# Second attention: one rounding and one subtraction for both heads, the halves moved by transfers

## The chip, the cores and the metric

The kernel runs on one core of a Trainium2 chip. The metric is the device time of one execution in microseconds; lower is better.

## What is computed

One inference step of a one-layer decoder: a prompt of 1024 rows and 8 sample rows with a paged cache of 8192 positions each. What matters here is the causal attention of the prompt with a forget gate, 8 heads of width 64:

```python
def fox_attend(q, k, v, cq, ck, qpos, kpos):
    s = jnp.einsum('bqhd,bkhd->bhqk', q, k).astype(jnp.float32) * (ATT_HEAD_DIM ** -0.5)
    s = s + (cq.astype(jnp.float32).transpose(0, 2, 1)[:, :, :, None]
             - ck.astype(jnp.float32).transpose(0, 2, 1)[:, :, None, :])
    s = jnp.where(kpos[None, :] <= qpos[:, None], s, -jnp.inf)
    p = jax.nn.softmax(s, axis=-1).astype(v.dtype)
    return jnp.einsum('bhqk,bkhd->bqhd', p, v)
```

Around it stand an input projection, a gating branch, an output projection, cross-attention into 256 memory tokens and a gated MLP with a convolution, for the prompt and for the samples.

## The kernel before

The prompt is worked in two halves of 512 rows. After the input projections (`p1`) comes the first attention (`attention(0)`: rows 0 to 511), then the second (`attention(1)`: rows 512 to 1023 against all 1024 keys), then for each half the merge, the output projection, cross-attention and the MLP. The samples' work, above all the reading of 128 pages of keys and 128 of values (L1420 and L1482, issued on POOL), is strewn into the prompt's by a pacing loop; DVE multiplies and reduces the key pages (in the attentions in quarters, L1427 and L1428), PE multiplies the value pages (L1488).

Matrices in float32 are split for PE into a rounded part h (type fp32r) and a rest l = x - h. For the scores, queries and keys of a head are laid out so that two matmuls do three products: `qq[:, 0, :]` holds the rounded queries in partitions 0 to 63 and their rests in 64 to 127, and `ka` holds the rounded keys twice, in both halves of the partitions (L807). `qq[:, 1, :]` holds the rounded queries again in 0 to 63, `kb` the keys' rests there, and partitions 64 to 67 of both carry the forget sums, loaded from `cq_d` and `ck_d` (L809).

An attention goes over four pairs of heads. `load` fetches a pair's queries (`qn`, one buffer), keys (`kn`) and values (`vn`) on SP's queue; in the second attention `kn` is a tile of the pool `t2` (7 buffers, shared with the outputs, some of the turned probabilities, and others). `setup` is a generator with one stop: the first step transposes the queries of both heads at once into one PSUM bank (L750) and rounds (ACT, L757), copies (POOL, L758) and subtracts (DVE, L774) head by head; the second does the same for keys (L779, L784, L785, L788). In the PSUM bank head 0 lies in partitions 0 to 63 and head 1 in 64 to 127. The first attention stores the split keys in `ks_d` in memory (L791, L792), and the second loads them from there for its first 512 keys (L769, L770, on SP), so that its setup only splits the 512 new ones. The operands `qq`, `ka` and `kb` are tiles of the pool `u` (18 buffers).

For a pair, `scores` is called eight times (two blocks of query rows, two heads, two row tiles); each call makes the scores on PE in column chunks, the row maximum on DVE (L813, L816), and the exponential on ACT (L814, L817; in the second attention into a `wr` tile, the buffers that also take weights). `turn` transposes the probabilities (PE L836, ACT L843 or DVE L841), `values` multiplies them with the values (L852), `back` transposes the result (L872, L874). The next pair's `load` is called after the first call of `scores`, its `setup` begins after the fourth, and its second step follows one call later.

Each engine takes its instructions in order. The order is made when the program is built, by a scheduler that uses an estimate of each instruction's time; `tc.issue_after` and `behind` add edges to it (`calm()` puts the rounding after the latest exponential). Transfers on SP's queue take turns on eight completion semaphores, and a transfer is issued only when the one eight before it, on the same semaphore, has landed.

Of the kernel before, what the change touches and what calls it, by code (L numbers as in the profile page):

```python
# [7 lines left out]
F32 = mybir.dt.float32  # L8
F32R = mybir.dt.float32r
BF16 = mybir.dt.bfloat16  # L10
I32 = mybir.dt.int32
AF = mybir.ActivationFunctionType
ALU = mybir.AluOpType
# [65 lines left out]
def build(nc, tc, ctx, a, phases=None):  # L79
# [27 lines left out]
    def nm(s):  # L107
        cnt[0] += 1
        return f"{s}_{cnt[0]}"

    def U(shape, dt=F32):
        n = 1
        for s in shape[1:]:
            n *= s
        t = upool.tile([P, UW], dt, tag="u", bufs=NU, name=nm("u"))[:, :n]
        if len(shape) == 3:
            t = t.rearrange("p (a b) -> p a b", b=shape[2])
        return t

    def T2(n=512, dt=F32):  # L120
        return tpool.tile([P, 512], dt, tag="t2", bufs=NT, name=nm("t2"))[:, :n]
# [604 lines left out]
    def attention(hf, late=None, at=3):  # L726
# [3 lines left out]
        def load(hp):  # L730
# [9 lines left out]
            nc.sync.dma_start(vn, v_d[: nk * P, cs].rearrange("(i p) c -> p i c", p=P))  # L740
            return qn, kn, vn

        def setup(hp, qn, kn, vn):


            calm = lambda: tc.issue_after(lastexp[0]) if lastexp else nullcontext()
            with behind(ENG.PE):
                tr = (MS, BB, BA)[SB]()
                for i in range(4):
                    nc.tensor.transpose(tr[:, i * P : (i + 1) * P], qn[:, i, :], ident)  # L750
            qab, ka, kb = [], [], []
            for j in range(2):
                h = hp * 2 + j
                rows = slice(64 * j, 64 * j + 64)
                qq = U([P, 2, 512], F32R)
                with calm():
                    nc.scalar.activation(qq[0:64, 0, :], tr[rows, :], AF.Copy)  # L757
                nc.gpsimd.tensor_copy(qq[0:64, 1, :], qq[0:64, 0, :].bitcast(F32))  # L758
                nc.gpsimd.dma_start(qq[64:68, 1, :], cq_d[h, :, hf * 512 : (hf + 1) * 512])
                qab.append(qq)  # L760
                if hf == 0:
                    kab = U([P, 2, 512], F32R)
                    ka.append(kab[:, 0, :])
                    kb.append(kab[:, 1, :])
                else:
                    ka.append(U([P, nk * P], F32R))
                    kb.append(U([P, nk * P], F32R))
                    for r in range(2):
                        nc.sync.dma_start(ka[j][64 * r : 64 * r + 64, 0:512].bitcast(F32), ks_d[h, :, 0, :])  # L769
                    nc.sync.dma_start(kb[j][0:64, 0:512].bitcast(F32), ks_d[h, :, 1, :])  # L770
                nc.gpsimd.dma_start(kb[j][64:68, :], ck_d[h, :, : nk * P])
            for j, qq in enumerate(qab):
                rows = slice(64 * j, 64 * j + 64)
                nc.vector.tensor_tensor(qq[64:128, 0, :], tr[rows, :], qq[0:64, 0, :].bitcast(F32), op=ALU.subtract)  # L774
            yield
            with behind(ENG.PE):
                tr = (MS, BB, BA)[SB]()
                for i in range(4):
                    nc.tensor.transpose(tr[:, i * P : (i + 1) * P], kn[:, i, :], ident)  # L779
            s = slice(hf * 512, hf * 512 + 512)  # L780
            for j in range(2):
                rows = slice(64 * j, 64 * j + 64)
                with calm():
                    nc.scalar.activation(ka[j][0:64, s], tr[rows, :], AF.Copy)  # L784
                nc.gpsimd.tensor_copy(ka[j][64:128, s], ka[j][0:64, s].bitcast(F32))  # L785
            for j in range(2):
                rows = slice(64 * j, 64 * j + 64)
                nc.vector.tensor_tensor(kb[j][0:64, s], tr[rows, :], ka[j][0:64, s].bitcast(F32), op=ALU.subtract)  # L788
            if hf == 0:
                for j in range(2):  # L790
                    nc.gpsimd.dma_start(ks_d[hp * 2 + j, :, 0, :], ka[j][0:64, :].bitcast(F32))  # L791
                    nc.gpsimd.dma_start(ks_d[hp * 2 + j, :, 1, :], kb[j][0:64, :].bitcast(F32))  # L792
            got.append((qab, ka, kb, vn))
# [92 lines left out]

        got = []
        first = setup(0, *load(0))
        if hf:
            next(first)  # L890
# [5 lines left out]
        for hp in range(4):  # L896
# [5 lines left out]
            for blk in range(2):  # L902
# [6 lines left out]
                for j in range(2):  # L909
                    for ii in range(2):  # L910
                        p_ = scores(qkv, ls, blk, j, ii)
                        if ii == 0:
                            pt.append(
                                [
                                    (U([P, 4, 256]) if nkt - g > 2 else T2(512).rearrange("p (a b) -> p a b", b=256))
                                    for g in range(0, nkt, 4)
                                ]
                            )
                        queue.append(partial(turn, p_, pt[j], nkt - 1 + ii, ii))
                        if j == 1 and ii == 1:  # L920

                            def fin(*args):
                                r = values(*args)
                                queue.insert(min(BKQ, len(queue)), partial(back, *r))

                            queue.append(partial(fin, qkv, ls, pt, hp, blk))
                        drain(LA[hf])
                        yield 1.8
                        if hp < 3 and (blk, j, ii) == LD[hf]:
                            raw = load(hp + 1)  # L930
                        if hp < 3 and (blk, j, ii) == ST[hf]:
                            nxt = setup(hp + 1, *raw)
                        if nxt:
                            next(nxt, None)
                            yield 1
# [425 lines left out]
    def behind(e):  # L1361

        return tc.issue_after(last[e]) if e in last else nullcontext()
# [480 lines left out]
    def prompt():  # L1844
# [4 lines left out]

        got, ahead = [], []  # L1850
        att1 = attention(1, lambda: got.append(merge_in(0)))
        att0, fill0 = attention(0, (lambda: next(att1)) if LT < 4 else None, LT), fill()

        def early():
# [170 lines left out]
```

## Time and profile before

| | us |
|---|---|
| median of 3 runs | 1805.22 |
| lowest and highest | 1799.28, 1807.2 |
| profiled execution, device time | 1804.14 |
| its span, first to last instruction | 1802.1 |
| PE busy in the span | 1737.0 |
| DVE busy | 1398.2 |
| ACT busy | 736.4 |
| POOL busy | 506.6 |

The mean granted TensorE clock is 0.991 of full speed. The page has the busy share of each engine, the span in 40 slices, the DMA queues, the chain of work that ended last and the costliest groups. Finer views answer for a stretch, a line or a tile. In them a group's row gives the line, engine, operation, output and inputs, the count, and the duration of one in ns; a wait's row gives who waited for whom, the total in us, the count and the longest; a timeline row gives the start, the length, the instruction and, in brackets, the idle time before it with what ended it. A row of a timeline with x2 stands for two instructions one after the other.

### The profile page before, as it was taken

The page shows a single profiled execution, that of the slowest core. Times are in us where ns is not written, and L with a number is a line of the kernel's source. Part 1 is how long each engine was busy: PE and PEld are TensorE (multiplying, and loading weights), DVE is VectorE, ACT ScalarE, POOL GpSimd, SP SyncE. Part 2 cuts the span into 40 slices and gives each one's busy share as a digit, 9 for nine tenths or more (in the row PEclk, how much of TensorE's full clock was granted, in tenths as well). Part 3 has the DMA queues.
Part 4 walks back from the last instruction along what each step waited for, and adds up shares of the span by engine and source line. Part 5 has one row for each costly group of instructions (what it writes and reads, how often), then busy time and mean ns, then how long its engine had stood idle before and what let it go on. Part 6 is the DMA issues. An engine that isn't in the chain of part 4 may idle for free.

```text
span 1802.1 us, 25097 instructions
## 1 busy us (share of the span) xinstructions
PE 1737.0 (96%) x9637; PEld 1287.2 (71%) x9637; DVE 1398.2 (78%) x1729; ACT 736.4 (41%) x1378; POOL 506.6 (28%) x461
## 2 busy tenths in 40 slices
PE   8999999878999999999999999999989999999997
PEld 5887777555677667777777777776666778767875
DVE  4689658988788986999999999887875549855344
ACT  6332265465643635333333244336353323332332
POOL 1252333433123332332322223343422112002110
PEclk9999999999999999999999999999999999999999
DMA  8886888786697985778788778988879687568982
GB/s 296 301 298 226 300 317 329 265 273 212 223 407 277 355 331 217 290 291 341 296 305 309 290 302 321 377 304 325 308 276 338 224 297 249 185 260 299 357 312 82
DMA packets 157074, 521.06 MB, mean 289 GB/s; under 512 B 20874, under 2 KB 40842, under 8 KB 124186
## 3 DMA queue, kind: packets, MB, share of 16 engines
q0 software_dynamic: 57168, 341.14, 49.8%
q1 hardware_dynamic: 92874, 165.73, 26.7%
q10 hardware_dynamic: 6912, 12.59, 1.9%
q8 instruction: 76, 1.25, 0.3%
q14 instruction: 44, 0.36, 0.1%
HBM read 495.47 MB, written 23.93 MB: 288 GB/s over the span
## 4 chain that ended last, share of the span: by engine, by line
PE 47%; DMA 11%; issue 8%; DVE 6%; POOL 2%; ACT 1%; POOLq 0%; DVEq 0%
DMA kv<-cache_v,io 7%; PE ba L272 6%; PE ba L274 6%; PE ba L273 6%; PE dv L1488 3%; PE bb L272 3%; PE bb L274 3%; PE bb L273 3%; DMA kv<-cache_k,io 2%; DVE s L1440 2%; DVE kv L1436 1%; PE dv L331 1%; PE dv L1764 1%; POOL kv L1482 1%; POOL kv L1420 1%
## 5 line engine op out<-in xcount | busy, mean ns | idle before, releaser
L235 ACT ACTIVATE wh<-wr 128x1024 fp32r<-128x1024 f32 (+2 forms) x220 | 228.9, 1044 | 421.5 <-PE ba L273 138.8
L236 DVE TENSOR_TENSOR wl<-wr,wh 128x1024 fp32r<-128x1024 f32 (+2 forms) x220 | 262.9, 1199 | 172.6 <-PE ba L274 57.7
L1420 POOL DMA_INDIRECT kv<-cache_k,io x128 | 199.2, 1556 | 570.9 <-DVE s L1440 325.3
L1436 DVE TENSOR_TENSOR kv<-kv,d 128x1024 f32<-128x1024 f32 (+1 forms) x156 | 258.1, 1681 | 24.7 <-DMA kv<-cache_k,io 24.7
L1440 DVE TENSOR_REDUCE s<-kv 128x16 f32<-128x1024 f32 (+1 forms) x156 | 258.1, 1672 | 0.0
L1482 POOL DMA_INDIRECT kv<-cache_v,io x128 | 168.5, 1317 | 254.9 <-PE dv L1488 177.5
L272 PE MATMUL ba<-u,wh 128*128 128x512 f32 x528 | 209.3, 397 | 0.0
L273 PE MATMUL ba<-u,wh 128*128 128x512 f32 x528 | 208.8, 396 | 0.5 <-DVE u L239 0.5
L274 PE MATMUL ba<-u,wl 128*128 128x512 f32 x528 | 208.8, 396 | 0.0
L272 PE MATMUL ba<-wh,u 128*128 128x512 f32 (+1 forms) x495 | 186.4, 379 | 2.6 <-ACT u L235 2.6
L273 PE MATMUL ba<-wl,u 128*128 128x512 f32 (+1 forms) x495 | 185.1, 375 | 1.2 <-DVE wl L236 1.2
L274 PE MATMUL ba<-wh,u 128*128 128x512 f32 (+1 forms) x495 | 183.2, 375 | 0.0
L1488 PE MATMUL dv<-kv,s 128*32 128x512 f32 x1024 | 127.7, 606 | 3.6 <-DMA kv<-cache_v,io 3.5
L272 PEld LDWEIGHTS ba<-u,wh 128*128 128x128 f32 x528 | 99.5, 188 | 27.2 <-issue 5.6
L274 PEld LDWEIGHTS ba<-u,wl 128*128 128x128 f32 x528 | 99.3, 188 | 26.5 <-issue 4.0
L273 PEld LDWEIGHTS ba<-u,wh 128*128 128x128 f32 x528 | 99.3, 188 | 25.8 <-issue 3.1
L272 PEld LDWEIGHTS ba<-wh,u 128*128 128x128 f32 x495 | 93.0, 188 | 27.0 <-issue 6.5
L272 PE MATMUL bb<-u,wh 128*128 128x512 f32 x272 | 108.7, 400 | 0.0
L274 PE MATMUL bb<-u,wl 128*128 128x512 f32 x272 | 107.8, 397 | 0.0
L273 PE MATMUL bb<-u,wh 128*128 128x512 f32 x272 | 107.6, 396 | 0.0
L273 PEld LDWEIGHTS ba<-wl,u 128*128 128x128 f32 x495 | 93.0, 188 | 20.0 <-DVE wl L236 1.9
L274 PEld LDWEIGHTS ba<-wh,u 128*128 128x128 f32 x495 | 92.9, 188 | 19.5 <-issue 1.6
(445 smaller groups left out, 3313.8 us busy)
## 6 DMA issues: line engine op xcount, KB each, us to landing
wr<-w_up SPq DMA_DIRECT2D x88, 512.0 KB
kv<-w_up POOLq DMA_DIRECT2D x22, 1024.0 KB, 7.6
wr<-w_down SPq DMA_DIRECT2D x40, 512.0 KB
kv<-w_down POOLq DMA_DIRECT2D x11, 1024.0 KB, 8.3
wr<-w_in SPq DMA_DIRECT2D x16, 512.0 KB
wr<-w_o SPq DMA_DIRECT2D x16, 512.0 KB
wr<-w_cq SPq DMA_DIRECT2D x16, 512.0 KB
wr<-w_co SPq DMA_DIRECT2D x16, 512.0 KB
```

The source lines that it names most:

```text
L235: nc.scalar.activation(h, src, AF.Copy)
L236: nc.vector.tensor_tensor(l, src, h.bitcast(F32), op=ALU.subtract)
L272: mmul(out, sh, mh, start=(i == 0), stop=False)
L273: mmul(out, sh, ml, start=False, stop=False)
L274: mmul(out, sl, mh, start=False, stop=(i == n - 1))
L331: mmul(ps[32 * j : 32 * j + 32, :w], xT[:, k, :] if nk == 8 else xT[:, k * 8 : k * 8 + 32], raw[:, q, j * w : (j + 1) * w], start=(k == 0) ...
L1420: nc.gpsimd.indirect_dma_start(kv, None, a["cache_k"], off(kidx[:, b, ch : ch + 1]))
L1436: nc.vector.tensor_tensor(kvv[:, i : i + m, :], kvv[:, i : i + m, :], qb.unsqueeze(1).broadcast_to((P, m, 512)), op=ALU.mult)
L1440: nc.vector.tensor_reduce(s[:, ch * 4 + i : ch * 4 + i + m, :].rearrange("p k h -> p (k h)"), kvv[:, i : i + m, :].rearrange("p k (h d) -> ...
L1482: nc.gpsimd.indirect_dma_start(kv, None, a["cache_v"], off(kidx[:, b, ch : ch + 1]))
L1488: mmul(dv[32 * j : 32 * j + 32, :], s[:, ch * 4 : ch * 4 + 4, :].rearrange("p k h -> p (k h)"), kvv[:, j, :], start=(ch == 1), stop=(ch == ...
L1764: mmul(ps[32 * j : 32 * j + 32, :P], xsT[:, k, :], rvs[j // 2][:, k, j % 2, :], start=(k == 0), stop=(k == 7), tile_position=(0, 32 * j),)
```

## The change

In the second attention only (`hf` is 1), `setup` no longer works head by head. A new helper `halves` rounds the whole PSUM bank, both heads, in one ACT instruction over 128 partitions, back into the tile that held the rows before the transpose (`qn` or `kn`), and subtracts in one DVE instruction into a new tile of the pool `t2`. Twelve transfers a pair on SP's queue, six for queries and six for keys, each of 64 partitions of 512 elements, bring the parts to their places in `qq`, `ka` and `kb`. The copies on POOL are gone there. The first attention is as it was.

```diff
+        def halves(tr, rows_, calm):
+
+            h = rows_.rearrange("p i c -> p (i c)")
+            with calm():
+                nc.scalar.activation(h.bitcast(F32R), tr, AF.Copy)
+            l = T2(512, F32R)
+            nc.vector.tensor_tensor(l, tr, h, op=ALU.subtract)
+            return h, l.bitcast(F32)
+
         def setup(hp, qn, kn, vn):
...
             qab, ka, kb = [], [], []
+            if hf:
+                qh, ql = halves(tr, qn, calm)
             for j in range(2):
                 h = hp * 2 + j
                 rows = slice(64 * j, 64 * j + 64)
                 qq = U([P, 2, 512], F32R)
-                with calm():
-                    nc.scalar.activation(qq[0:64, 0, :], tr[rows, :], AF.Copy)
-                nc.gpsimd.tensor_copy(qq[0:64, 1, :], qq[0:64, 0, :].bitcast(F32))
+                if hf:
+                    for dst, part in ((qq[0:64, 0, :], qh), (qq[0:64, 1, :], qh), (qq[64:128, 0, :], ql)):
+                        nc.sync.dma_start(dst.bitcast(F32), part[rows, :])
+                else:
+                    with calm():
+                        nc.scalar.activation(qq[0:64, 0, :], tr[rows, :], AF.Copy)
+                    nc.gpsimd.tensor_copy(qq[0:64, 1, :], qq[0:64, 0, :].bitcast(F32))
...
-            for j, qq in enumerate(qab):
+            for j, qq in enumerate(() if hf else qab):
                 rows = slice(64 * j, 64 * j + 64)
                 nc.vector.tensor_tensor(qq[64:128, 0, :], tr[rows, :], qq[0:64, 0, :].bitcast(F32), op=ALU.subtract)
             yield
...
             s = slice(hf * 512, hf * 512 + 512)
+            if hf:
+                kh, kl = halves(tr, kn, calm)
             for j in range(2):
                 rows = slice(64 * j, 64 * j + 64)
+                if hf:
+                    for dst, part in ((ka[j][0:64, s], kh), (ka[j][64:128, s], kh), (kb[j][0:64, s], kl)):
+                        nc.sync.dma_start(dst.bitcast(F32), part[rows, :])
+                    continue
                 with calm():
                     nc.scalar.activation(ka[j][0:64, s], tr[rows, :], AF.Copy)
                 nc.gpsimd.tensor_copy(ka[j][64:128, s], ka[j][0:64, s].bitcast(F32))
-            for j in range(2):
+            for j in range(0 if hf else 2):
                 rows = slice(64 * j, 64 * j + 64)
                 nc.vector.tensor_tensor(kb[j][0:64, s], tr[rows, :], ka[j][0:64, s].bitcast(F32), op=ALU.subtract)
```

## The prediction

> **What bounds the kernel now.** I read the page first, then busy time by stage, then the second attention alone: its waits, its costs, its transfers, and the hand-over from one pair of heads to the next. On the page the tensor engine fills the span:
>
> ```profile
> span 1802.1 us, 25097 instructions
> PE 1737.0 (96%) x9637; PEld 1287.2 (71%) x9637; DVE 1398.2 (78%) x1729; ACT 736.4 (41%) x1378; POOL 506.6 (28%) x461
> ```
>
> Busy time by stretch (length, then PE, PEld, DVE, ACT and POOL busy, granted clock, DMA share, GB/s) shows where PE still has holes:
>
> ```profile
> 340.00:490.00 150.00, 128.30 (x904) 89.61 (x902) 124.14 (x227) 95.52 (x216) 44.98 (x62) 0.98 0.68 222
> 490.00:700.00 210.00, 206.92 (x1057) 150.34 (x1051) 183.51 (x228) 94.32 (x198) 75.48 (x50) 1.00 0.87 330
> 380.00:400.00 20.00, 17.10 (x110) 11.61 (x108) 19.63 (x34) 11.67 (x23) 10.08 (x14) 0.92 0.87 244
> 420.00:440.00 20.00, 15.10 (x95) 11.21 (x92) 16.34 (x26) 9.12 (x18) 4.10 (x6) 0.91 0.77 229
> 440.00:460.00 20.00, 18.74 (x141) 12.96 (x138) 15.14 (x26) 12.72 (x28) 7.24 (x10) 1.00 0.79 273
> ```
>
> The second attention lies at about 340 to 490 us. There PE is idle for 150 - 128.3 = 21.7 us, against 3.1 us in the 210 us after it. All that the change can win lies in those 21.7 us; what it makes late there is passed on, since the next stage has no room. The waits of 360 to 490 us (waiter, releaser: total, times, longest) say what ended PE's holes:
>
> ```profile
> PE ba L807 <- ACT wr L817: 6.8, 6, 1.9
> PE bb L836 <- ACT wr L817: 3.6, 3, 1.5
> PE ms L836 <- ACT wr L817: 2.2, 2, 1.2
> ```
>
> PE waits 6.8 + 3.6 + 2.2 = 12.6 us for the exponential, which follows the row maximum on DVE. So a shorter DVE and ACT queue can pay. No wait of PE for a transfer stands near the top: operands are in time today.
>
> **The edits on the engines.** Durations, min/median/max in ns:
>
> ```profile
> L757 ACT ACTIVATE u<-ba x16: 577/591/600, 239.8 to 446.8; 64x512 fp32r<-64x512 f32 x16
> L843 ACT ACTIVATE u<-bb x39: 481/597/620, 286.7 to 486.5; 128x512 f32<-128x512 f32 x26, 128x384 f32<-128x384 f32 x13
> L774 DVE TENSOR_TENSOR u<-ba,u x16: 683/690/695, 242.0 to 448.4; 64x512 fp32r<-64x512 f32 x16
> L1427 DVE TENSOR_TENSOR kv<-kv,d x64: 656/681/1052, 269.0 to 499.4; 128x512 f32<-128x512 f32 x64
> L785 POOL CAST u<-u x16: 604/609/717, 243.0 to 453.7; 64x512 fp32r<-64x512 f32 x16
> ```
>
> Half of each x16 belongs to the second attention (four pairs of heads, two heads each). An operation on 128 partitions costs what one on 64 costs: 0.597 beside 0.591 us on ACT, 0.681 beside 0.690 on DVE. So ACT goes from 16 roundings to 8 and saves 8 x 0.59 = 4.7 us; DVE goes from 16 subtractions to 8 and saves 8 x 0.69 = 5.5 us; POOL loses 16 copies of 0.61 = 9.8 us. Together ACT and DVE give back 10.2 us. If none of it stands in front of a row maximum or an exponential the gain is 0; if all does, 10.2. I take 4: PE's wait on that chain is 12.6 us of 130, so most of the time a late ACT or DVE is covered by PE's own work, and 4 is the part of 10.2 that I give to the rest, a choice nearer the lower end. POOL's 9.8 us I cost at nothing: no hole of PE above ends with a copy or a page, so a page asked for a few us sooner meets no waiting PE.
>
> **The edits on SP's queue.** Each setup puts 12 more transfers of 64 x 512 elements (128 KB) on SP: three a head for queries, three a head for keys. Those of ks_d have the same size and are the nearest rows. First the issue, then one seen from issue to landing, then the traffic of 340 to 500 us (packets, MB, share of 16 engines):
>
> ```profile
> L769 SPq DMA_DIRECT2D u<-ks_d x16: 445/587/1471, 355.4 to 442.6; - x16
> ...
> 417.14 0.70 SPq L770 DMA_DIRECT2D u<-ks_d  x1
> ...
> 421.91 1.02 POOL L1420 DMA_INDIRECT kv<-cache_k,io  x1 [1.55 <-DMA u<-ks_d]
> ...
> q1 hardware_dynamic: 14421, 14.82, 31.3%
> u<-ck_d POOLq DMA_DIRECT2D x8, 16.0 KB, 7.5
> ...
> DMA to landing us min/median/max: 2.3/5.0/8.5
> ```
>
> POOL was released at 421.9 by the ks_d load issued at 417.1, so a 128 KB load takes L = 4.8 us here; the stores into ks_d (last line) span 2.3 to 8.5, and small loads in the same stretch take 7.5. Price of the extra traffic: 14.82 MB cost 31.3% of 160 us, 50.1 us, or 0.296 MB per us; 12 x 0.131 MB are 5.3 us of all engines at each setup. At 380 to 400 us the DMA share leaves 2.6 of 20 us, at 420 to 440 4.6, at 440 to 460 4.2. All three overflow by 0.7 to 2.7 us, so L grows; I take 7, about 2 above the one load seen, and keep 4.8 and 8.5 as bounds. A transfer inside SBUF doesn't occur in the trace; that it is much quicker than one from memory I can't exclude, hence 4.8 as a live end.
>
> The program adds a second limit: SP's transfers take turns on eight semaphores, and each waits for the one eight before it. In the changed order a setup is 18 in a row: three of queries, three of ks_d, again three and three, then six of keys. The lower half of the first head's keys is the 15th. So it starts not before the 15th slot of 0.59 us, nor before the 7th has landed, and lands L later.
>
> Now the time there is. Key subtraction (DVE L788) and first score using it (PE L807), pair by pair; between them the query operations of three pairs, one pair's query transposes (L750) and a run of value matmuls (L852):
>
> ```profile
> 366.12 1.40 DVE L788 TENSOR_TENSOR u<-ba,u 64x512 fp32r<-64x512 f32 x2
> 375.79 0.39 PE L807 MATMUL ba<-u,u 128*128 128x320 f32 x1
> ...
> 385.34 1.20 ACT L757 ACTIVATE u<-ba 64x512 fp32r<-64x512 f32 x2
> 388.04 1.41 DVE L774 TENSOR_TENSOR u<-ba,u 64x512 fp32r<-64x512 f32 x2
> 392.33 1.38 DVE L788 TENSOR_TENSOR u<-ba,u 64x512 fp32r<-64x512 f32 x2
> 401.33 0.39 PE L807 MATMUL ba<-u,u 128*128 128x320 f32 x1
> 412.92 0.60 PE L750 MATMUL ba<-cp,qn 128*128 128x128 f32 x4
> 418.73 1.39 DVE L774 TENSOR_TENSOR u<-ba,u 64x512 fp32r<-64x512 f32 x2
> 433.18 0.39 PE L807 MATMUL ba<-u,u 128*128 128x320 f32 x1
> ...
> 446.18 1.21 ACT L757 ACTIVATE u<-ba 64x512 fp32r<-64x512 f32 x2
> 450.72 1.72 PE L852 MATMUL bb<-u,u 128*64 128x256 f32 x13
> 453.28 1.39 DVE L788 TENSOR_TENSOR u<-ba,u 64x512 fp32r<-64x512 f32 x2 [1.45 <-issue]
> 459.58 0.39 PE L807 MATMUL ba<-u,u 128*128 128x320 f32 x1
> ```
>
> Today operands lie ready 8.3, 7.6 and 4.9 us ahead in the first, second and fourth pair. The changed order of PE helps: it sets the first column chunk of the scores, which needs old keys only, ahead and puts up to nine value matmuls and some transposes before the second chunk: 9 x 1.72/13 = 1.2 us and a little less again for the transposes, about 2 us of cover. Counting on today's clock:
> - Fourth pair: rounded queries at 446.8; 7th transfer at 450.3, 15th at 455.1 or at 450.3 + L. With L = 7 it starts at 457.3 and lands at 464.3; needed at 459.6 + 2 = 461.6; late by 2.7. With 4.8: not late. With 8.5: 5.7.
> - Second pair: the third transfer waits for the subtraction, 388.7; 7th at 391.1; with L = 7 the 15th lands at 405.1, needed at 403.3, late by 1.8 (0 and 4.8 at the bounds).
> - Third pair: third at 419.4, 7th at 421.8, landing 435.8, needed 435.2, late by 0.6 (0 and 3.6).
> - First pair: its keys stand behind two stores of the gating; about 375 against 375.8, late by 0 (0 and 0.7).
>
> Sum: 5.1 us (0 and 14.8). A wait here holds PE, which takes its queue in order: behind the late score stand the transposes and value matmuls of the pair before, and behind those DVE's maxima and ACT. Behind the waiting SP stands the next pair's query load, now after all 18. In the second pair the 18th goes out at 400.5 with L = 7 (the 2nd at 386.5, the 10th after it has landed at 393.5, the 18th after that one), the load lands at about 408, and the transposes that want it run at 412.9: hidden with 4.8 us to spare, at L = 8.5 with nothing.
>
> The clock adds to it: 380 to 400 us ran at 0.92, 1.6 us of 20 lost after a hole in PE's work. I add one such loss, 1.6 us (0 to three of them, 4.8). The Trainium skill ("TensorE: Matmul & The Clock Gate", HAM clock gate) says the clock halves after an idle window of about 3.4 us; by that rule stalls under 3 us would cost no clock and the sum would be 1.6 us less.
>
> Everything after 490 us is the same work in a slightly different order, PE's holes there being small (3.1 in 210 us); I cost this at 0, with about 5 us either way over 1312 us.
>
> Sum on the profiled execution: -4 + 5.1 + 1.6 = +2.7 us on 1804.14 us (span 1802.1 plus 2.0 around it). That execution lies 1.1 below the median of 1805.22, so about 1808 us. A measurement of this kernel can tell about 0.5%, 9 us, from no change.
>
> **Rivals.**
>
> Late halves (slower): L is 8.5, since the bursts fall on a DMA share of 0.87 already and eight in flight make L count twice. PE then stands 14.8 us, three slow-clock stretches add 4.8, the saving takes back 4: +15.6, 1821 us. It decides from L of about 8 on. For it: the overflow computed above and the 7.5 us of small loads. Against it: the seen 4.8.
>
> Engines relieved (faster): L stays at 4.8 or less, nothing is late, and nearly all of ACT's and DVE's 10.2 us lay before exponentials: -10, 1795 us. For it: 12.6 us of PE waiting on just that chain, DVE at 19.63 of 20 us in one setup. Against it: the overflow, and the slack of DVE in the other stretches. The Trainium skill ("DMA: Bandwidth & Descriptors", Anatomy of one DMA) gives about 2 us plus bytes over 436 GB/s, some 2.3 us for 128 KB, as an estimate from that page; by it nothing would be late and this rival gains; the 4.8 us seen above do not agree with it, in a loaded stretch. If the relief lies wholly off the path, the result is 0 to +7 us, inside the forecast.
>
> **How the numbers follow.** Forecast 0.42 (own range 1800 to 1814), late halves 0.36, engines relieved 0.22. The forecast lies within 0.5% of before, late halves are slower by over 9 us, engines relieved faster by over 9 us or near it; so faster 0.22, same 0.42, slower 0.36. The range takes in both rivals' central times with the 5 us of reordering on the slow side: 1795 to 1826.
>
> **What would show it.** In the profile after: one 128-partition rounding and subtraction per round at about 0.6 and 0.69 us; 48 more SP transfers of 128 KB, 6.3 MB; DMA share near 1 in the setups; PE waiting on transfers from qn and the t tiles, 2 to 3 us at a hand-over, the fourth pair the worst; waits of PE on the exponential down by some 4 us. Landings under 5 us with no such wait, or waits of 5 us and over at several pairs, would make it wrong; so would a change of over 5 us that arises after 490 us.

## The result and the profile after

| | before | after |
|---|---|---|
| median of 6 runs each, same chip | 1802.16 us | 1830.9 us |
| lowest and highest | 1797.95, 1807.2 | 1823.5, 1835.78 |
| ratio, 95% interval | | 1.0155 (1.0133 to 1.0177) |
| profiled execution | 1804.14 us | 1835.78 us |

The change costs 28 us. The forecast was 1808, its range ended at 1826. The profiled execution of the kernel after is the slowest of its six, so sizes read from it lie some 5 us above the median.

The page of the kernel after, engines and granted clock in 40 slices:

```profile
span 1833.9 us, 25158 instructions
PE 1753.7 (96%) x9637; PEld 1299.8 (71%) x9637; DVE 1392.5 (76%) x1721; ACT 731.8 (40%) x1370; POOL 492.5 (27%) x445
...
PEclk9999999987899999999999999999999999999999
```

ACT and DVE did save: 731.8 for 736.4, and 1392.5 for 1398.2. But PE needs 1753.7 us in place of 1737.0 for the same 9637 products: 16.7 of the 31.8 us by which the span grew are not idle time, they are PE running slower. The other 15.1 are holes. Three slices of the clock row show where. Busy time by stretch (PE, PEld, DVE, ACT, POOL, then clock, DMA share, GB/s) of the kernel after:

```profile
340.00:490.00 150.00, 113.02 (x706) 78.90 (x708) 99.33 (x187) 71.54 (x168) 33.55 (x43) 0.85 0.78 221
360.00:380.00 20.00, 11.59 (x71) 8.60 (x70) 8.83 (x20) 8.61 (x26) 3.34 (x4) 0.78 0.99 314
440.00:460.00 20.00, 10.49 (x48) 6.86 (x48) 9.04 (x15) 5.54 (x10) 1.56 (x2) 0.75 1.05 268
```

Against 0.98 before, the second attention ran at 0.85, with 706 products started in 150 us where there were 904. That the whole loss is here is seen from the first load of the next stage's weights. The row gives the first and last start of a group; first the kernel before, then after, stretch 300 to 560 us:

```profile
L249 SPq DMA_DIRECT2D wr<-w_o x8: 367/373/1452, 480.8 to 507.8; - x8
```

```profile
L249 SPq DMA_DIRECT2D wr<-w_o x8: 368/378/2099, 512.1 to 536.6; - x8
```

The stage ends 31.3 us later, and the span is 31.8 longer. What holds PE in it, from the waits of 360 to 520 us of the kernel after (total, times, longest):

```profile
PE ba L828 <- ACT wr L838: 8.4, 4, 5.8
PE bb L893 <- ACT t L882: 8.4, 3, 7.5
ACT t L835 <- DMA u<-t: 7.6, 1, 7.6
PE ba L828 <- DMA u<-t: 6.1, 2, 4.5
PE bb L857 <- ACT wr L838: 5.6, 4, 2.3
PE ba L830 <- DMA u<-ks_d: 2.9, 2, 2.2
PE ba L828 <- DMA u<-ks_d: 2.2, 2, 2.0
PE ba L830 <- DMA u<-t: 1.1, 1, 1.1
```

(L828 and L830 are the score products, L835 an exponential of the first attention, L838 one of the second, L857 and L893 transposes.) PE waits 12.3 us for transfers, and none of these waits stood in the trace before. A further 7.6 us is an exponential that waits for a transfer out of a `t` tile, and PE behind it. In order of time, ACT's row first, then PE's:

```profile
373.39 0.69 ACT L835 ACTIVATE t<-ba,mx 128x512 f32<-128x512 f32 x1 [7.55 <-DMA u<-t]
```

```profile
375.39 0.69 PE L893 MATMUL bb<-cp,t 128*128 128x128 f32 x2 [7.49 <-ACT t L882]
390.18 0.63 PE L828 MATMUL ba<-u,u 128*128 128x320 f32 x1 [5.80 <-ACT wr L838]
...
412.54 1.76 PE L857 MATMUL bb<-cp,wr 128*128 128x128 f32 x7 [2.35 <-ACT wr L838]
416.50 0.61 PE L828 MATMUL ba<-u,u 128*128 128x320 f32 x1 [1.67 <-DMA u<-t]
...
445.69 0.38 PE L828 MATMUL ba<-u,u 128*128 128x320 f32 x1 [1.98 <-DMA u<-ks_d]
457.75 0.93 PE L828 MATMUL ba<-u,u 128*128 128x320 f32 x2 [4.47 <-DMA u<-t]
486.34 0.38 PE L830 MATMUL ba<-u,u 68*128 68x320 f32 x1 [2.25 <-DMA u<-ks_d]
```

The exponential of the first attention writes into one of the seven `t2` buffers. In the changed order that buffer had held the first setup's query rests, so the exponential may not write until their transfer has read them. The rows that name a transfer are late operands, with every pair but the first.

The 5.80 us ahead of 390.18 are neither. They end with the first exponential of the second attention, which waits for its row maximum. DVE takes that maximum (L837) only behind the first half's merge, whose factor `rar` (L222) and four scalings (L979) wait for the tail of the first attention, and that tail had been held by the 7.5 us:

```profile
385.46 0.17 DVE L222 TENSOR_SCALAR rar<-ssa 128x4 f32<-128x4 f32 x1 [1.41 <-ACT junk L230]
386.80 1.67 DVE L979 TENSOR_SCALAR u<-u,rar 128x512 f32<-128x512 f32 x4 [1.16 <-POOL rar L223]
388.39 0.82 DVE L837 TENSOR_REDUCE mx<-ba 128x1 f32<-128x640 f32 x1
```

The scores of that tile were there at 384.1. In the kernel before, the scheduler had put the same maximum ahead of the merge:

```profile
376.47 0.81 DVE L816 TENSOR_REDUCE mx<-ba 128x1 f32<-128x640 f32 x1
...
379.27 0.16 DVE L222 TENSOR_SCALAR rar<-ssa 128x4 f32<-128x4 f32 x1
...
381.86 1.67 DVE L958 TENSOR_SCALAR u<-u,rar 128x512 f32<-128x512 f32 x4
```

There the hole at this place was 1.89 us. So most of this hole comes from an order of DVE's instructions that the change brought with it. How long a transfer took stands in the chain of waits (start, length), second and third pair:

```profile
408.12 8.24 DMA u<-t
...
433.96 12.49 DMA u<-ks_d
446.47 11.14 DMA u<-t
```

And the clock behind such holes, in stretches of 4 us of the kernel after:

```profile
372.00:376.00 4.00, 0.61 (x3) 0.61 (x4) 0.90 (x1) 2.61 (x8) 0.00 (x0) 0.50 1.03 389
376.00:380.00 4.00, 4.00 (x17) 3.39 (x16) 1.26 (x5) 2.63 (x7) 0.00 (x0) 0.50 0.98 241
408.00:412.00 4.00, 2.19 (x15) 1.58 (x14) 4.00 (x7) 1.21 (x2) 2.81 (x3) 1.00 0.97 287
412.00:416.00 4.00, 2.29 (x9) 1.89 (x9) 3.93 (x7) 2.56 (x6) 0.00 (x0) 0.53 1.02 319
416.00:420.00 4.00, 3.50 (x15) 3.26 (x15) 1.51 (x3) 1.27 (x2) 1.51 (x2) 0.50 1.03 308
```

After the hole of 7.5 us PE had half the clock in the next stretch too: 376 to 380 is full of work (4.00) and at 0.50.

### The profile page after: what moved, and what is told of

Same layout as the page of the kernel before. It is cut to its first block, busy times and chain, and to the rows that moved or that the text cites. A ratio compares the mean times of both kernels' runs of the same rounds, so it can differ in the third digit from the quotient of the medians.

```text
span 1833.9 us, 25158 instructions
## 1 busy us (share of the span) xinstructions
PE 1753.7 (96%) x9637; PEld 1299.8 (71%) x9637; DVE 1392.5 (76%) x1721; ACT 731.8 (40%) x1370; POOL 492.5 (27%) x445
## 4 chain that ended last, share of the span: by engine, by line
PE 52%; DMA 10%; DVE 9%; issue 8%; ACT 2%; POOL 2%; SPq 0%; POOLq 0%; DVEq 0%; ACTq 0%
PE ba L272 6%; PE ba L274 6%; PE ba L273 6%; DMA kv<-cache_v,io 5%; PE dv L1509 4%; PE bb L272 3%; PE bb L274 3%; PE bb L273 3%; DVE kv L1457 2%; DVE s L1461 2%; DMA u<-t 1%; PE ba L1086 1%; PE ba L1085 1%; PE ba L1087 1%; DVE wl L236 1%
## 5 line engine op out<-in xcount | busy, mean ns | idle before, releaser
L1441 POOL DMA_INDIRECT kv<-cache_k,io x128 | 191.2, 1493 | 572.9 <-DVE s L1461 321.3
L274 PEld LDWEIGHTS ba<-u,wl 128*128 128x128 f32 x528 | 99.3, 188 | 27.3 <-issue 4.8
```

The costliest lines, as they stand in the source:

```text
L274: mmul(out, sl, mh, start=False, stop=(i == n - 1))
L1441: nc.gpsimd.indirect_dma_start(kv, None, a["cache_k"], off(kidx[:, b, ch : ch + 1]))
```

## The experiments

Theory T: late transfers hold scores and exponentials, and each hold is paid again in slow clock. Rivals: A, the load on engines and queue whoever waits; B, the small `t2` buffers; C and D, the changed order of instructions that the scheduler makes; Q, the order on SP's queue. Every ratio is to the kernel before on the same chip, with its 95% interval.

**One half of the change at a time.** e1 keeps the query edit and takes back the key edit, e2 the reverse.

```diff
 # e1
-            if hf:
-                kh, kl = halves(tr, kn, calm)
...
-                if hf:
-                    for dst, part in ((ka[j][0:64, s], kh), ...):
-                        nc.sync.dma_start(dst.bitcast(F32), part[rows, :])
-                    continue
```

> Queries go by halves and transfers, keys are made as before: 24 of the 48 added transfers, and none of keys. Theory (late transfers hold the scores and the exponential, and each hold is paid again in a slow clock): the first pair's 7.5 us hold of the exponential on the query rests stays, and so do the loads of the stored keys that stand behind the query transfers (5.1 us of PE waits); the waits on key transfers (11.4 us of PE and weight loads) go. About half of the 29 us: 1812 to 1820 us. Rival A (it is the load on the transfer engines and the queue, whoever waits): half of the bytes, about the same 1815. Rival B (the rests in the small rotating tiles hold the exponential): nearly all stays, 1825 or more. Rival C (a changed order of the instructions): no relation to the number of transfers.

> Keys go by halves and transfers, queries are made as before. Theory: the waits of PE on the key transfers stay in pairs 2 to 4, the hold of the exponential in the first pair goes, the stored keys' loads are not behind anything: 1808 to 1820 us. Rival A: as the queries alone, about 1815. Rival B: near 1805, since the query rests are not in a small tile.

Measured: queries 1.0048 (1.0032 to 1.0063), keys 1.0053 (1.0025 to 1.0082). Each alone costs about 9 us, a third of the loss where T expected about half, though both times (1812.5 and 1815.5) lie in its ranges; together the two edits cost 1.55%, half as much again as the sum. PE's waits of the keys alone are on their transfers:

```profile
376.40 0.61 PE L822 MATMUL ba<-u,u 128*128 128x320 f32 x1 [6.06 <-DMA u<-t]
410.07 0.63 PE L824 MATMUL ba<-u,u 68*128 68x320 f32 x1 [2.96 <-DMA u<-t]
443.11 0.61 PE L822 MATMUL ba<-u,u 128*128 128x320 f32 x1 [2.68 <-DMA u<-t]
```

B, by which the queries would hold nearly all, falls as the whole cause. But the cost does not follow PE's waits: on moved parts and stored keys they sum to 14.0 us with the keys alone and to 0.9 with the queries alone, at the same loss. With the queries alone the exponential's hold is there too, 4.6 us.

**The same transfers, waited for by nobody.** e4 is the kernel before, plus 12 transfers a setup into unused rows.

```diff
+                    for dst in (kb[j][68:128, 0:512], kb[j][68:128, 512:1024], qq[68:128, 1, :]):
+                        nc.sync.dma_start(dst.bitcast(F32), qq[0:60, 0, :].bitcast(F32))
...
+                for dst, part in ((kb[j][68:128, 0:512], ka[j][0:60, s]), ...):
+                    nc.sync.dma_start(dst.bitcast(F32), part.bitcast(F32))
```

> The kernel before, with 12 transfers a setup beside its work: 60 x 512 elements each, inside SBUF, on the same queue at the same places, into rows that nothing reads. The same count and 94% of the bytes, but no score waits for them. Theory: only what stands behind them on the queue suffers (stored keys 2 to 4 us at some pairs): 1804 to 1812 us. Rival A (load and queue alone): 1822 to 1831 us, as the change.

Measured: 1.0031 (1.0011 to 1.0052). The stretches of e4 show engines as full as in the change:

```profile
360.00:380.00 20.00, 14.80 (x103) 10.18 (x103) 14.91 (x32) 13.34 (x38) 5.65 (x9) 0.98 1.00 297
380.00:400.00 20.00, 16.76 (x110) 11.41 (x108) 19.17 (x33) 10.64 (x22) 10.37 (x13) 0.93 1.06 263
```

So the load itself is worth 0.3%, a fifth of the loss, and A falls as the main cause. The rest must come with the parts being needed or with the order that this brings; e4 does not tell these two apart.

**The halves without a transfer.** e3 lets GpSimd copy all 12 parts, f2 does it for queries alone, keys as before.

```diff
-                        nc.sync.dma_start(dst.bitcast(F32), part[rows, :])
+                        nc.gpsimd.tensor_copy(dst, part[rows, :])
```

> The halves are made as in the change, but GpSimd copies them to their operands (12 copies of about 0.61 us a setup, 4 before) and no transfer is added. Theory: with no late transfer the loss goes, and the relief of the two engines shows as far as it is worth anything: 1795 to 1806 us. Rival C (order): stays above 1820. If rounding and subtracting both heads at once is itself harmful (a longer chain from the transposes to the operands), 1808 to 1815.

> Queries alone go by halves, copied to their operands by GpSimd; keys as before; no transfer added. Theory T: no operand is late, one chain fewer on ACT and DVE: 1798 to 1805 us. Theory D: the planner's order differs from before about as much as in the change, half or more of the 17 us of both by GpSimd: 1810 to 1820.

Measured: e3 1.0100 (1.0070 to 1.0130), f2 1.0056 (1.0038 to 1.0073). T failed here: it gave 1795 to 1806 and the copies took 1821. That is where the order's rivals had put them: C above 1820 for e3, and D 1810 to 1820 for f2, which took 1812.6. Without any added transfer two thirds of the loss stays, and queries by GpSimd cost as much as queries by transfers. In e3's fourth pair the hop waits again, now in GpSimd's queue behind page requests. POOL's row, then PE's:

```profile
477.50 3.13 POOL L802 CAST u<-t 64x512 fp32r<-64x512 f32 x4 [3.14 <-DMA kv<-cache_k,io]
```

```profile
480.01 0.42 PE L830 MATMUL ba<-u,u 68*128 68x320 f32 x1 [3.39 <-POOL u L802]
```

That is the only direct wait of PE on a copy, 3.4 us. Its wait on the second attention's exponential is 18.0 us (12.6 before), though ACT and DVE have less to do:

```profile
PE ba L828 <- ACT wr L838: 6.5, 3, 3.3
PE bb L857 <- ACT wr L838: 6.4, 6, 1.6
PE ms L857 <- ACT wr L838: 5.1, 5, 1.6
```

**Is it the order?** The scheduler, counting with later operands, sets the first score chunks of a pair ahead and the second back. f1 imposes this on the kernel before; h2 (on e3) and h3 (on the change) forbid it by an edge.

```diff
 # f1
+            chunk(0)
+            if hf and blk == 0 and j == 0:
+                held_.append((chunk, soft))
+                if ii == 1:  # then chunk 1, maximum and exponential of both tiles
 # h2, h3
+                with tc.issue_after(lastsc[0]) if lastsc else nullcontext():
+                    mmul(s, qab[j][:, 0, i * P : (i + 1) * P], ...)
...
+                lastsc[:] = [newest(ENG.PE)]
```

> The kernel before, engines and transfers unchanged; only the order of PE is shifted as the planner shifts it in the change: in each pair's first block the first chunks of both score tiles of the first head go ahead, the second chunks follow, so the first exponential of the pair comes later. Theory D (the copies by GpSimd cost 1.0% without any transfer, since the planner counts with later operands and sets the scores in another order): slower by 8 to 17 us, 1810 to 1820. Theory T (only late operands cost): within 4 us of before, 1800 to 1808.

> The copies by GpSimd without any added transfer, and each score tile's first product is put behind the last product of the tile before it on PE, so the planner can't set the first chunks ahead and the second chunks back. Theory D (the interleaved order of the chunks costs most of the 1.0%): 1804 to 1812 us. If it is the hop itself (GpSimd's copies behind its page requests, operands later): 1816 to 1824, with PE's wait on a copy still there.

> The change with the same edge. Theory D: the part that lies in the order goes, 1818 to 1825 us. If late landings set the start of each pair's scores: 1828 or more, since the first chunk of the second tile, which needs older keys, can no longer go while the first tile waits.

Measured: f1 1.0041 (1.0024 to 1.0059); h2 1.0112 (1.0087 to 1.0138); h3 1.0165 (1.0139 to 1.0191). Without the interleaving neither kernel is faster, so D falls for both as far as the order of the chunks on PE goes; the edge does not touch DVE's order, and in h2 and h3 the merge's `rar` still stands ahead of the first row maximum. h3 is at the time that T gave. f1 shows that another order can cost 0.4% by itself, but in its profile the next stage's load starts at 479.2 us, 1.6 earlier than before, so that cost arises later, and where is not settled.

**More time.** f3 starts each setup of the change one turn sooner, f4 the same in the kernel before.

```diff
-ST = [(0, 1, 1), (0, 1, 1)]
+ST = [(0, 1, 1), (0, 1, 0)]
```

> The change, with every setup of the second attention started one turn sooner (the loads stay). Theory T: the transfers get some 5 us more before their scores, which takes most of the holds in pairs 2 to 4: 1808 to 1818 us. If the buffers that the setup takes sooner hold other work instead, or the holds come from the load on the engines: 1826 or more. To be read against the next run.

> The kernel before with the same sooner start: the control. Its operands are in time already: 1800 to 1808 us by either theory; a loss here is the price of the sooner start itself.

Measured: f3 1.0115 (1.0087 to 1.0142), f4 1.0045 (1.0032 to 1.0058). Starting sooner costs the old kernel 0.45%. The new one comes out 0.4% below the change's ratio, with intervals that overlap a little, so the difference between the two kernels falls from 1.55% to 0.7%. The time is above what T gave, by about the control's price, which was not foreseen. But the trace does not bear T out: PE waits 14.4 us for transfers in f3, more than the 12.3 us in the change, and the exponential's hold is 8.9 us. So what the sooner start relieved was not these waits.

**Remedies.** g1 puts the rests into a large buffer, g2 moreover loads the stored keys first, g3 leaves the duplicates to GpSimd (8 transfers a setup), g4 issues the transfers on ACT.

```diff
 # g1, g2
-            l = T2(512, F32R)
+            l = U([P, 512], F32R)
 # g3, and the same for ka[j][64:128, s]
-                    for dst, part in ((qq[0:64, 0, :], qh), (qq[0:64, 1, :], qh), (qq[64:128, 0, :], ql)):
+                    for dst, part in ((qq[0:64, 0, :], qh), (qq[64:128, 0, :], ql)):
                         nc.sync.dma_start(dst.bitcast(F32), part[rows, :])
+                    nc.gpsimd.tensor_copy(qq[0:64, 1, :], qh[rows, :])
 # g4
-                        nc.sync.dma_start(dst.bitcast(F32), part[rows, :])
+                        nc.scalar.dma_start(dst.bitcast(F32), part[rows, :])
```

> The change, with the rests of a round in one of the 18 large rotating buffers in place of the 7 small ones, which the exponentials of the first attention, the values' results and the stored keys share. Theory B (buffer): the 7.5 us hold of the exponential in the first pair goes and with it some of the slow clock behind it: 1815 to 1825 us. If a hold in one place only moves lateness to the next (the operands are late at every pair): 1827 to 1833.

> As the run before in this list, and the loads of the stored keys of both heads stand ahead of the query transfers on the queue. Theory Q (queue): the 5.1 us of waits of PE on stored keys go as well, 5 to 10 us below the run with large rests alone. If the burst as a whole is late (load on the engines), the wait moves to the query or key transfers: within 4 us of it.

> The change with 8 transfers a setup in place of 12: GpSimd copies the second set of rounded rows (4 copies of 0.61 us a setup, as before the change). A third of the added bytes goes and the last transfer of a setup is the 14th, not the 18th. Theory T: landings come sooner, a third or more of what the transfers add over the copies by GpSimd goes: 1820 to 1826 us. If GpSimd's copies stand behind its page requests (as in the run with GpSimd copies in the fourth pair), no gain or a loss: 1828 to 1836.

> The change with the 48 transfers issued by ACT in place of SP, so that loads of stored keys and the next pair's rows stand behind none of them. Theory Q: the waits on stored keys go, the key transfers land sooner; ACT pays the issue (12 a setup), and what it waits for the subtraction holds its exponentials: between 1815 and 1830 us. If the load on the engines decides, no better than the change: 1828 or more, and the waits on transfers stay.

Measured: g1 1.0140 (1.0105 to 1.0176), g2 1.0128 (1.0088 to 1.0168), g3 1.0103 (1.0072 to 1.0135), g4 1.0143 (1.0107 to 1.0178). g1, g2 and g4 can't be told from the change. In g1 the hold of the exponential is gone, and PE waits for the transfers instead:

```profile
380.49 0.92 PE L828 MATMUL ba<-u,u 128*128 128x320 f32 x2 [4.80 <-DMA u<-t]
444.67 0.60 PE L828 MATMUL ba<-u,u 128*128 128x320 f32 x1 [2.55 <-DMA u<-t]
449.62 0.63 PE L830 MATMUL ba<-u,u 68*128 68x320 f32 x1 [4.36 <-DMA u<-u]
```

So taking away the hold of B or of Q alone gains nothing that can be told; the wait moves to the next place. g4 was no better although its transfers left SP's queue: ACT, which now issues them, stands idle 20.8 us ahead of three exponentials of the second attention until a transfer has landed. Fewer transfers (g3) came out lower, at about what GpSimd's copies cost, though its interval just overlaps the change's. PE's waits on moved parts are down to 4.6 us there, and 1.0% of loss stays.

**The relief by itself.** h1 leaves the second head's operations out of the kernel before.

```diff
-                with calm():
-                    nc.scalar.activation(qq[0:64, 0, :], tr[rows, :], AF.Copy)
-                nc.gpsimd.tensor_copy(qq[0:64, 1, :], qq[0:64, 0, :].bitcast(F32))
+                if not (hf and j):
+                    with calm():
+                        nc.scalar.activation(qq[0:64, 0, :], tr[rows, :], AF.Copy)
+                    nc.gpsimd.tensor_copy(qq[0:64, 1, :], qq[0:64, 0, :].bitcast(F32))
...  # likewise the subtractions and the keys
```

> The kernel before, in whose second attention the second head's rounding, copy and subtraction are left out (8 roundings, 8 subtractions, 8 copies), and both heads' scores are made from the first head's operands; all loads stay. So ACT and DVE lose just as many operations as by the change, and nothing is added. If the relief is worth what the prediction gave it: -4 us, 1799. If all of it stands in front of exponentials: -10, 1793. If PE's own work covers it, or the planner's other order takes it back: 0 to +8, 1803 to 1811.

Measured: 0.9989 (0.9976 to 1.0003), -2.0 us (-4.3 to +0.5). If the relief is worth as much in the change, parts that reached their operands for nothing would have won it about 2 us and hardly more than 4. h1 has an order of its own and still copies the duplicates of the first head, so this is an estimate.

**Where each profile lost.** Against the profile of before, in us: growth of the span, of PE's busy time, what remains as holes, and the shift of the next stage's first load. The last column is what PE waited itself, from 340 to 535 us, for a transfer or a GpSimd copy into an operand (0 before). Each row is a single execution, and executions of one kernel differ by some us.

| | span | PE busy | holes | shift | PE's waits |
|---|---|---|---|---|---|
| the change | +31.8 | +16.7 | +15.1 | +31.3 | 12.3 |
| e1 queries by transfers | +11.2 | +10.8 | +0.4 | +8.3 | 0.9 |
| e2 keys by transfers | +12.3 | +10.7 | +1.6 | +16.3 | 14.0 |
| e3 all by GpSimd | +15.9 | +5.9 | +10.0 | +15.1 | 3.4 |
| e4 idle transfers | +2.7 | +0.2 | +2.5 | +5.9 | 0.2 |
| f1 late chunks | +4.8 | +0.3 | +4.5 | -1.6 | 0 |
| f2 queries by GpSimd | +10.5 | +6.1 | +4.4 | +3.8 | 0 |
| f3 the change, sooner | +20.7 | +3.9 | +16.8 | +24.8 | 14.4 |
| f4 before, sooner | +9.3 | +11.2 | -1.9 | +11.8 | 0 |
| g1 rests in large buffers | +21.6 | +5.8 | +15.8 | +19.7 | 14.0 |
| g2 and stored keys first | +17.3 | +11.1 | +6.2 | +23.2 | 10.6 |
| g3 duplicates by GpSimd | +10.8 | +6.8 | +4.0 | +13.0 | 4.6 |
| g4 on ACT's queue | +24.8 | +13.8 | +11.0 | +27.3 | 0.5 |
| h2 GpSimd, with the edge | +14.2 | +10.5 | +3.7 | +12.3 | 2.2 |
| h3 the change, with the edge | +28.4 | +8.6 | +19.8 | +26.4 | 11.6 |

The split into holes and slow clock varies, and the loss does not follow PE's own waits. f1, f2 and f4 lose 0.4 to 0.6% with none; e2 loses no more with 14.0. So a loss of about 0.5% needs no late transfer: an order or a timing of the second attention other than in the kernel before is enough.

## Why the prediction was wrong

The mechanism forecast (transfers behind full engines land late, PE stands at the hand-over, the clock falls) is seen in the trace of the change, and the direction of its sum was right. Two of its terms were far too small, the landing and the clock, and it had no term for the buffer hold or for the changed order on DVE. How much of the 28 us each of these makes is not shown. By its steps:

- **Operations saved, and their durations.** Right: 0.611 us for a 128-partition rounding (0.59 for the first attention's shape), 0.682 for a subtraction. These rows are of the kernel after:

```profile
L747 ACT ACTIVATE qn<-ba x4: 600/611/623, 355.6 to 470.3; 128x512 fp32r<-128x512 f32 x4
L749 DVE TENSOR_TENSOR t<-ba,qn x4: 679/682/691, 357.0 to 471.0; 128x512 fp32r<-128x512 f32 x4
```

- **The relief, -4 of 10.2.** Too much: -2.0 by h1, whose interval just holds -4. PE's waits on the second attention's exponential, which were to fall by some 4 us from 12.6, are 14.3 us from 360 to 520 us of the kernel after.
- **The landing, L = 7.** The step that failed first. It was taken from one load in a quieter place (4.8) with 2 us put on, although the same paragraph computes that three setups overflow. Measured in the second and third pair: 8.2 and 11.1 us; the stored keys' load in the same burst 12.5. The lower bound, 4.8, came from a stage whose share of the engines was 0.68; in bursts of the changed kernel's setups it is 0.97 to 1.05. The upper, 8.5, is the longest of the stores into `ks_d`, which run from 243.5 to 354.8 us, for the most part in the first attention, and it too was passed.
- **Lateness, 0, 1.8, 0.6 and 2.7 a pair, sum 5.1.** PE's waits on transfers sum to 12.3: 1.7 in the second pair, 7.1 in the third, 3.6 in the fourth, stored keys included, which the prediction did not count though it put their loads behind the query transfers. The fourth was not the worst. The first pair's 0 is right for operands and wrong for the stage: 7.5 us by the `t2` buffer and 5.8 by the row maximum behind the merge (1.9 before), waits the prediction had no term for. The rests were a new tenant of a pool of seven, and their stay lasts until the transfer has read them.
- **Clock, 1.6 (0 to 4.8).** The term most out: PE's busy time grew by 16.7 us. It counted one short loss, but there is a slow stretch at nearly every hold. The Trainium skill ("TensorE: Matmul & The Clock Gate", HAM clock gate), read as saying that stalls under 3 us cost no clock, does not agree: from 408 to 420 us the longest hole is 2.35 us, and the clock there went to 0.53 and 0.50.
- **Copies taken off POOL, 0.** Nothing contradicts it. **The next query load, hidden.** Right: no product waits for one. **After 490 us, 0 with 5 either way.** Right: the span grew 0.5 us more than the shift at the stage's end.
- **Estimate by a page.** The Trainium skill ("DMA: Bandwidth & Descriptors", Anatomy of one DMA) has a fit, by which the prediction estimated 2.3 us for 128 KB; the page gives it for transfers issued by GpSimd, and these were issued on SP. The 8.2 and 11.1 us do not agree, and the measurement decides. The estimate made the rival of relieved engines look stronger.
- **The rival "late halves"** came nearer, at 1821 us by L = 8.5. It lacked the stored keys, the buffer, the order on DVE and most of the clock.

What stays open: the shares of the causes, and why the copies by GpSimd cost 1.0% when PE waits for them 3.4 us. Of the scheduler's order, only the interleaving of the chunks was tried apart. The traces point at one more place: with GpSimd's copies too, `rar` stands ahead of the first row maximum on DVE. In e3 that maximum begins 1.8 us after its scores, in place of 0.1 us before, and PE's hole there is 3.29 us in place of 1.89. No run puts that order back by itself, so what it costs is not shown. Nor is it settled whether e3 and the change lose for the same reason. What is shown is partial: the load by itself costs 0.3% (e4), the halves with GpSimd's copies and no added transfer 1.0% (e3), and transfers in place of these copies about 0.55% more.

## What to carry to other kernels

Before a step between engines is replaced by transfers, ask what it wins if they cost nothing (here about 2 us, by h1), and then what an extra hop costs at the hand-over, in whatever queue it stands. Price the landing under the load that the change itself makes, not by a load seen in a quieter place, and count the buffers that a transfer keeps until it has read them. Read the order of every engine again after the change: here a row maximum slipped behind another stage's work. Holes of PE have a price in clock besides: in the change's profile 15 us of holes came with 17 us more of busy time, but in the other runs the relation was quite different, so no factor can be given.

## What was not expected of the hardware

- A transfer of 128 KB within SBUF took 8.2 and 11.1 us from issue to release, with the 16 engines at a share of 0.97 to 1.05 in the stretches around; the same count of transfers that nobody waits for costs 0.3%.
- The clock was granted at about half (0.53 and 0.50) in the two stretches of 4 us after one in which PE was busy 2.19 of 4 us and no hole was over 2.35, and for the 8 us from 372 to 380 around the end of a hole of 7.5.
- The granted clock differed between executions of the same program: 0.979 in the slowest of the six after (span 1833.9), 0.985 in the fastest (1821.7). Over the six, the slower ones mostly have the lower clock.
